# Gate columns by one full transposition a tile, products on all rows, and the sample read as the last 32 of 128 tokens

## The chip, the cores and the metric

The kernel runs on one core of a Trainium2 chip. The metric is the device time of one execution in microseconds (us), the median of several runs; lower is better. The engines are TensorE (PE in the profile, PEld for its loads of the stationary operand), VectorE (DVE), ScalarE (ACT), GpSimd (POOL) and SyncE (SP), which issues the DMAs.

## What is computed

One step of a streaming encoder layer for two streams at once: 1024 tokens of a new stream (the prompt) and the next 32 tokens of a running one (the sample). The mixer has three groups of heads, each a recurrence over the tokens that is computed in chunks; behind it comes a feed-forward part with a causal convolution. The reference, cut to what the change touches:

```python
proj = xn @ w_in                       # xn: (tokens, 1024)
(gq, gk, gv, gg, gr, hq, hf, hi, hg, mq, mk, mv, mi, mf, mo) = jnp.split(proj, pts, axis=-1)
log_a = log_sigmoid(gg @ gla_w_gate + gla_b_gate) / GLA_GATE_NORM      # gg: 16 columns
...
ig = mi + ml_b_i                       # 5 columns: input gate of the mLSTM heads
log_fm = log_sigmoid(mf + ml_b_f)      # 5 columns: forget gate
...
dc = jnp.exp(b[:, -1] + m - m_last)    # decay of a head's state over a chunk
c_new = dc[..., None, None] * c + jnp.einsum('bjh,bjhk,bjhv->bhkv', wk, kc, vc)
```

## The kernel before

**Tiling.** Tokens are worked on in three groups of 384, 384 and 256 prompt tokens, the last with the 32 sample tokens behind them (288 columns). A tile of tokens ("unit" u) has 128 tokens; the sample is unit 8 with n = 32. The function inproj makes the projections of a group: products with features in rows (pf, lines 350 and following), and products with tokens in rows (pv, lines 420 to 430). All large products are made of three passes over operands that are split into a high and a low part (mm3, lines 88 to 91), so lines 89, 90 and 91 carry most of TensorE's stream.

**Gate columns.** The first token-row product of a unit has 282 columns: 256 values, 16 gate columns gg, and 5 + 5 of the mLSTM gates. Line 428 copies the last 26 to tgs (tokens in rows, 26 columns a unit). Lines 471 to 473 turn them: for each unit three products of tgs with the identity put 16 columns on rows 64 to 79 of tg, and 5 each on rows 96 and 32 onwards. Lines 474 to 476 copy these rows to gg (which shares its tile with the forget gate fm) and ig.

**Products with few rows.** Line 529 multiplies gg (rows 64 to 79) with the gate weights into z0; line 604 does it for the other 64 channels into z3. Line 582 spreads the five decays dc over 128 rows. A product with few rows or columns uses a part of TensorE's array (a shape of rows x columns, such as 32x128 or 64x64).

**Mixers.** For each unit, mixer computes scores and states with many products of 64 rows and columns (line 776, sc, um, sm, up, og, oh). Lines 762 to 766 transpose the decayed keys kh, lines 794 to 802 those of the mLSTM heads, and lines 958 to 962 take row sums (mi at line 672; the helper first at line 671 issues all of these). In group 2 the later token-row products are made the other way round and transposed back at line 438 (pb), also for the sample's 32 tokens. Line 1405 transposes the result of the last part.

**The order.** The program is written unit by unit, but function order at the end lets a list scheduler (play) put the instructions of every engine in a new order, by estimated costs and tail lengths. Its function choose decides when TensorE leaves the full shape for a smaller one: small products wait until 300 ns of them have come together (GATE) or one has waited for PATIENCE, 3000 ns. So an edit in one place moves instructions elsewhere.

## Time and profile before

| | |
|---|---|
| median of 3 runs | 1328.19 us (1327.99 to 1331.88) |
| the profiled execution's own time | 1327.83 us |
| its span, first to last instruction | 1326.0 us |
| TensorE, TensorE's loads | 1293.3 us, 1208.7 us (98%, 91%) |
| VectorE, ScalarE, GpSimd | 1034.2, 724.8, 181.1 us |
| DMA over the span | 285.25 MB, 215 GB/s |

The share of busy time says which engine is full: TensorE. A product's duration in the profile runs from its start to its modelled end, and products overlap, so the time that one takes in the stream is the distance from its start to the next start. In a row of the timeline stand start, duration, engine, line, operation, what it writes and reads, the size of the stationary operand (rows\*columns), the moving operand, and the count of rows that were merged; in brackets the engine's idle time before it and what ended it.

### The profile page before, as it was taken

Reading aid. Unit: us, or ns where it says so; the run is one execution under the profiler, and the core shown is the slowest. Engines: PE = TensorE matmul, PEld = TensorE weight load, DVE = VectorE, ACT = ScalarE, POOL = GpSimd, SP = SyncE. Lnnn points to the kernel's source line nnn. Section 1 sums busy time; section 2 is a strip of 40 time slices with the busy share of each in tenths; the row PEclk is TensorE's granted clock in tenths of the full one; section 3 lists DMA queues with packets and bytes.
Section 4 is the critical chain, followed back from the end, with each engine's and each line's share of the span. In section 5 each row is a group of like instructions: output and inputs, shape, how many; then the busy total and the mean of one; then the engine's idle time right before and its main releaser. Section 6 shows DMA issues by size and latency. Waiting matters only on the chain. (4 is left out here: it accounts for less than half of the span.)

```text
span 1326.0 us, 30530 instructions
## 1 busy us (share of the span) xinstructions
PE 1293.3 (98%) x12005; PEld 1208.7 (91%) x12005; DVE 1034.2 (78%) x1877; ACT 724.8 (55%) x1432; POOL 181.1 (14%) x331
## 2 busy tenths in 40 slices
PE   8999999999998999999999999999999999999997
PEld 7999999999898888778899999999999999888886
DVE  6795559748788478779899998888888878676686
ACT  6555566546576454436754545445454455365664
POOL 2020001111011112223112211111111110010010
PEclk9999999999999999999999999999999999999999
DMA  9899879977899863545256643222232268887774
GB/s 333 283 337 334 268 264 317 318 252 247 279 317 297 307 234 116 176 119 157 104 191 195 217 153 121 95 99 81 90 121 97 97 217 286 295 273 259 226 251 179
DMA packets 148455, 285.25 MB, mean 215 GB/s; under 512 B 30071, under 2 KB 84503, under 8 KB 148311
## 3 DMA queue, kind: packets, MB, share of 16 engines
q1 hardware_dynamic: 148311, 283.30, 63.7%
q8 instruction: 94, 1.54, 0.5%
q14 instruction: 50, 0.41, 0.1%
HBM read 201.90 MB, written 81.34 MB: 214 GB/s over the span
## 5 line engine op out<-in xcount | busy, mean ns | idle before, releaser
L1257 DVE SCALAR_TENSOR_TENSOR y<-uu,fconv_sb,y 128x1060 f32<-128x1060 f32 x88 | 116.0, 1321 | 7.7 <-ACT y L1255 6.7
L98 DVE TENSOR_TENSOR hlp<-rp,hhp 128x384 fp32r<-128x384 f32 x77 | 42.5, 555 | 35.3 <-PE pdw L91 11.3
L1255 ACT ACTIVATE y<-uu,fconv_sb 128x1060 f32<-128x1060 f32 x44 | 56.2, 1277 | 22.9 <-POOL uu L1252 17.1
L95 ACT CAST hhp<-rp 128x384 fp32r<-128x384 f32 x77 | 39.6, 515 | 49.0 <-PE pdx L90 18.2
L1203 ACT COPY c<-pux 128x274 f32<-128x274 f32 (+1 forms) x132 | 46.2, 380 | 27.1 <-PE pux L91 25.0
L933 POOL TENSOR_TENSOR hrs<-hss,mhalf 128x5 f32<-128x5 f32 (+3 forms) x27 | 36.1, 1340 | 163.8 <-DVE hss L932 162.8
L98 DVE TENSOR_TENSOR wdp<-rp,wdp 128x512 fp32r<-128x512 f32 x77 | 52.0, 688 | 3.7 <-ACT wdp L95 2.6
L89 PE MATMUL pv<-wt_0h,xh 128*128 128x256 f32 (+2 forms) x195 | 53.1, 294 | 1.4 <-ACT xh L311 0.6
L95 ACT CAST wdp<-rp 128x512 fp32r<-128x512 f32 x77 | 47.0, 621 | 10.1 <-PE pdx L91 3.4
L91 PE MATMUL pv<-wt_0h,xl 128*128 128x256 f32 (+2 forms) x195 | 50.6, 286 | 0.2 <-DVE xl L312 0.2
L90 PE MATMUL pv<-wt_0l,xh 128*128 128x256 f32 (+2 forms) x195 | 50.4, 284 | 0.2 <-DVE wt_0l L98 0.2
L91 PE MATMUL pv<-wt_1h,xl 128*128 128x256 f32 (+2 forms) x195 | 48.1, 287 | 0.0
L89 PE MATMUL pv<-wt_1h,xh 128*128 128x256 f32 (+2 forms) x195 | 47.2, 285 | 0.0
L90 PE MATMUL pv<-wt_1l,xh 128*128 128x256 f32 (+2 forms) x195 | 46.9, 285 | 0.0
L1252 POOL COPY uu<-fcache_sb 128x2 f32<-128x2 f32 x44 | 19.0, 431 | 185.8 <-DVE uu L1208 185.8
L91 PE MATMUL pdx<-wdp,hlp 128*128 128x512 f32 x132 | 43.2, 391 | 0.0
L90 PE MATMUL pdx<-wdp,hhp 128*128 128x512 f32 x132 | 43.0, 389 | 0.0
L89 PE MATMUL pdx<-wdp,hhp 128*128 128x512 f32 x132 | 42.7, 391 | 0.0
L1254 POOL COPY fhalo<-uu 128x2 f32<-128x2 f32 x44 | 35.7, 812 | 50.5 <-DVE uu L1208 49.9
L89 PEld LDWEIGHTS pv<-wt_0h,xh 128*128 128x128 f32 (+1 forms) x195 | 34.8, 187 | 2.8 <-ACT xh L311 0.9
L211 POOL TENSOR_SCALAR gss<-gss 128x1 f32<-128x1 f32 (+1 forms) x9 | 6.7, 747 | 216.6 <-ACT gjk L1331 132.5
L91 PEld LDWEIGHTS pv<-wt_0h,xl 128*128 128x128 f32 (+1 forms) x195 | 34.3, 187 | 1.0 <-issue 0.4
(1784 smaller groups left out, 5124.4 us busy)
## 6 DMA issues: line engine op xcount, KB each, us to landing
h_d<-y SPq DMA_DIRECT2D x22, 530.0 KB, 3.3
rp<-t_d SPq DMA_DIRECT2D x44, 256.0 KB, 3.9
wt_0r<-in_w_tok SPq DMA_DIRECT2D x21, 512.0 KB, 6.1
wt_1r<-in_w_tok SPq DMA_DIRECT2D x21, 512.0 KB, 5.5
rp<-in_w_dn SPq DMA_DIRECT2D x33, 256.0 KB, 4.2
rp<-s_d SPq DMA_DIRECT2D x44, 192.0 KB, 3.8
wt_0l<-lt_d SPq DMA_DIRECT2D x14, 512.0 KB, 5.0
wt_1l<-lt_d SPq DMA_DIRECT2D x14, 512.0 KB, 5.6
```

The source lines that it names most:

```text
L89: pe.matmul(ps, lh[0], rh[0], start=first, stop=False, **kw)
L90: pe.matmul(ps, lh[0], rh[1], start=False, stop=False, **kw)
L91: return pe.matmul(ps, lh[1], rh[0], start=False, stop=last, **kw)
L95: act.copy(hi, src)
L98: (eng or pool).tensor_tensor(lo, src, hi.bitcast(F32), op=ALU.subtract)
L211: pool.tensor_scalar(out, ss, other, EPS, op0=ALU.add, op1=ALU.add)
L933: pool.tensor_tensor(rs[:n, h0:h0 + nh], ss[:n, h0:h0 + nh], mhalf[:n, :nh], op=ALU.pow)
L1203: act.copy(t, ps)
L1252: pool.tensor_copy(u[:, GAP_S:GAP_S + 2], fcache[:, j, :])
L1254: pool.tensor_copy(fhalo[:, j, :], u[:, NCOL - 2:NCOL])
L1255: act.activation(y, u, AF.Identity, scale=fconv[:, j, 2:3], bias=fconv[:, j, 3:4])
L1257: dve.scalar_tensor_tensor(y, uu[i][:, s:s + NCOL], fconv[:, j, s:s + 1], y, op0=ALU.mult, op1=ALU.add)
```

## The change

The gate columns are kept as 128 columns a unit, zero but for the 26 in use, each set already at the column that will be its row: ScalarE copies 16 to columns 64 to 79, VectorE the other ten to columns 32 and 96 onwards, and GpSimd fills the tile with zeros first. One transposition a unit then writes all 128 rows of tg. The tile now uses the buffers of tag "q", two of them. The gate products read 96 rows (the weights of the other rows are zero) and write 128; the decay product reads 128 rows, with dc filled with zeros.

For the sample, products that read its 32 tokens now read 128 tokens, of which its own are the last 32 (in line 1405 and in the row sums the first 32), so that they use the full shape; the rest of the result is not read. Its keys are transposed at once, as 128 columns of four planes, and copied in four pieces. PATIENCE goes to 4000. The diff, cut:

```diff
         def vg_store(blk, u, off, n, ps):
+            r = slice(128 - n, 128)
...
-                act.copy(o[:n], ps[:n, :256])
-                sp.dma_start(v_d[t:t + n, 256 * blk:256 * blk + 256], o[:n])
+                act.copy(o[r], ps[r, :256])
+                sp.dma_start(v_d[t:t + n, 256 * blk:256 * blk + 256], o[r])
...
-                    mm3(ps[:n, :N], (xh[:, k, off:off + n], xl[:, k, off:off + n]), ws[k], k == 0, k == 7)
+                    mm3(ps, (xh[:, k, off + n - 128:off + n], xl[:, k, off + n - 128:off + n]), ws[k], k == 0, k == 7)
                 if not blk:
-                    act.copy(tgs[:n, i, :], ps[:n, 256:])
+                    act.copy(tgs[:, i, 64:80], ps[:, 256:272])
+                    dve.tensor_copy(tgs[:, i].rearrange("p (a b) -> p a b", b=64)[:, :, 32:37],
+                                    ps[:, 272:282].rearrange("p (a b) -> p a b", b=5))
...
-                        pe.transpose(ps[:n, 128 * e:128 * e + 128], fs[e][:, off:off + n], ident)
+                        pe.transpose(ps[:, 128 * e:128 * e + 128], fs[e][:, off + n - 128:off + n], ident)
...
-        tgs = pf.tile([128, 3, 26], F32, tag="tgs", name=f"tgs{g}")
+        tgs = pf.tile([128, 3, 128], F32, tag="q", name=f"tgs{g}", bufs=2)
+        pool.memset(tgs, 0.0)
...
-            for (r0, c0, c1) in ((64, 0, 16), (96, 16, 21), (32, 21, 26)):
-                pe.matmul(gt_[r0:r0 + c1 - c0, off:off + n], tgs[:n, i, c0:c1], ident[:n, :n], start=True, stop=True)
-        act.copy(gg[64:80], gt_[64:80, :T])
+            pe.transpose(gt_[:, off + n - 128:off + n], tgs[:, i], ident)
+        act.copy(gg[:96], gt_[:96, :T])
...
-        pe.matmul(z0[:, :T], wg[64:80, 0:128], gg[64:80, :], start=True, stop=True)
+        pe.matmul(z0[:, :T], wg[:96, 0:128], gg[:96], start=True, stop=True)
...
+            pool.memset(dc, 0.0)
...
-                pe.matmul(dcp[:, f, :ci], self_[R, 128 * f:128 * f + 128], dc[R, :ci], start=True, stop=True)
+                pe.matmul(dcp[:, f, :ci], self_[:, 128 * f:128 * f + 128], dc[:, :ci], start=True, stop=True)
...
-        pe.matmul(z3[:64, :T], wg[64:80, 128:192], gg[64:80, :], start=True, stop=True)
+        pe.matmul(z3[:, :T], wg[:96, 64:192], gg[:96], start=True, stop=True)
...
-        for f0 in (0, 2):
+        if u == 8:
+            kps = small(128)
+            pe.transpose(kps, khf, ident)
+            for f in range(4):
+                act.copy(kt[:n, 128 * f:128 * f + 128], kps[n * f:n * f + n])
+        for f0 in (0, 2) if u < 8 else ():
...
+        if u == 8:
+            dve.memset(z[:, 128:224], 0.0)
         for f in range(4):
-            first(pe.matmul, sd[:n], z[:, f * n:f * n + n], of_head[:, f, :], start=f == 0, stop=f == 3)
+            first(pe.matmul, sd, z[:, f * n:f * n + 128], of_head[:, f, :], start=f == 0, stop=f == 3)
...
-                    pe.transpose(pts[hf][:n, 128 * d:128 * d + 128], accs[4 * hf + d][:, off[u]:off[u] + n], ident)
+                    pe.transpose(pts[hf][:, 128 * d:128 * d + 128], accs[4 * hf + d][:, off[u]:off[u] + 128], ident)
...
-GATE, PATIENCE = 300., 3000.
+GATE, PATIENCE = 300., 4000.
```

Where TensorE's order moves, in three places. First, in group 0, the first gate columns (tg from tgs) behind the transpositions of the third unit's input (xt) and among that unit's token-row products (pv). Before (the last two rows then follow once more, for the second unit, and behind them line 91):

```order
L309 MATMUL xt_318<-ident,x_107 128x128 x4
L89 MATMUL pv_0_325<-wt_0_0h,xh_185 128x282
L90 MATMUL pv_0_325<-wt_0_0l,xh_185 128x282
L473 MATMUL tg_356<-ident,tgs_202 16x128
L473 MATMUL tg_356<-ident,tgs_202 5x128 x2
```

Now:

```order
L91 MATMUL pv_0_284<-wt_0_2h,xl_186 128x282
L309 MATMUL xt_321<-ident,x_107 128x128 x4
L89 MATMUL pv_0_328<-wt_0_0h,xh_185 128x282
L90 MATMUL pv_0_328<-wt_0_0l,xh_185 128x282
L91 MATMUL pv_0_328<-wt_0_0h,xl_186 128x282
```

The first gate transposition now stands nine rows further down, and the second some 26 rows behind that. Line 91, which reads xl, comes directly behind line 90.

Second, the end of the same group's last gate columns and the product z0 that reads them (pf are feature-row products). Before:

```order
L90 MATMUL pf_8_376<-xl_186,wf_8h 128x384
L91 MATMUL pf_8_376<-xh_185,wf_8l 128x384
L473 MATMUL tg_356<-ident,tgs_202 16x128
L473 MATMUL tg_356<-ident,tgs_202 5x128 x2
L529 MATMUL z_0_419<-r_fm_354,wg_sb 128x384
L89 MATMUL pf_6_433<-xh_185,wf_6h 128x384
```

Now:

```order
L90 MATMUL pf_8_374<-xl_186,wf_8h 128x384
L91 MATMUL pf_8_374<-xh_185,wf_8l 128x384
L476 MATMUL tg_360<-ident,tgs_202 128x128
L532 MATMUL z_0_417<-r_fm_358,wg_sb 128x384
L89 MATMUL pf_6_431<-xh_185,wf_6h 128x384
```

Three rows became one; z0 follows directly in both.

Third, the sample's keys (kh) in group 2, among token-row products pv, transpositions back (pb) and the sample's small products (sm). Before:

```order
L91 MATMUL pv_5_1_6621<-xh_4321,wt_5_1l 128x288
L672 MATMUL mi<-ident,kh_7017 32x128 x2
L438 MATMUL pb_4_6647<-ident,vf_6503 128x128 x2
L438 MATMUL pb_4_6655<-ident,vf_6503 32x128 x2
L776 MATMUL sm_7027<-mqk_6902 32x32 x3
L776 MATMUL sm_7028<-mqk_6902 32x32 x2
L89 MATMUL pv_6_0_6676<-xh_4321,wt_6_0h 128x288
```

Now:

```order
L441 MATMUL pb_5_6699<-ident,vf_6583 128x128
L90 MATMUL pv_6_0_6673<-xl_4320,wt_6_1h 128x288
L91 MATMUL pv_6_0_6673<-xh_4319,wt_6_1l 128x288
L768 MATMUL mi<-ident,kh_7014 128x128
L89 MATMUL pv_6_1_6707<-xh_4319,wt_6_0h 128x288
```

The keys' one transposition stands alone among wide products; the small products sm went to a later place, together with the sample's state products.

## The prediction

> **What bounds the kernel now.** I read the page first, then busy time by stage, then the waits of the engine that is full, and last the timeline of TensorE alone around every line that the change touches.

> ```profile
> span 1326.0 us, 30530 instructions
> PE 1293.3 (98%) x12005; PEld 1208.7 (91%) x12005; DVE 1034.2 (78%) x1877; ACT 724.8 (55%) x1432; POOL 181.1 (14%) x331
> ```

> The span is TensorE's: it is busy for 1293 of 1326 us. So an edit counts only as far as it shortens TensorE's stream of products or moves a wait in it. The profiled execution took 1327.83 us, 1.8 us more than its span and 0.36 us less than the median of the runs shown (1328.19); the sum below is made against 1327.83. A measurement of this kernel can tell about 0.3% (4 us) from no change, so the line for "faster" lies at 1324.2 and for "slower" at 1332.2.

> ```profile
> 0.00:400.00 400.00, 391.55 (x4594) 372.88 (x4595) 288.63 (x625) 238.52 (x471) 46.63 (x82) 1.00 0.88 296
> 400.00:480.00 80.00, 72.23 (x981) 65.61 (x980) 55.30 (x148) 45.02 (x111) 7.93 (x7) 0.98 0.83 278
> ```

> Each row has the stretch, its length, busy time and instructions of PE, PEld, DVE, ACT and POOL, then TensorE's granted clock (full, or 0.98 of it), the DMA engines' share and GB/s. TensorE is idle for 8.4 us of the first 400 and for 7.8 us of the 80 after that, where the sample's mixer runs and the DMA engines are 83% busy. Of the second half of the program the change touches eight transpositions (line 1405) and nothing else, so I look at the first. The waits that concern the change are short:

> ```profile
> PE pv L91 <- DMA wt_1l<-lt_d: 1.8, 1, 1.8
> PE tg L473 <- DVE xl L312: 1.4, 2, 0.9
> PE z L529 <- ACT r_fm L474: 0.7, 1, 0.7
> ```

> **Gate columns (lines 428 and 471 to 476).** Per tile three narrow products of two passes each go, and one transposition comes. In the timeline (start, duration) the next start shows what a row costs, since products overlap:

> ```profile
> 163.61 0.29 PE L90 MATMUL pv<-wt_2l,xh 128*128 128x282 f32 x1
> 163.74 0.29 PE L91 MATMUL pv<-wt_2h,xl 128*128 128x282 f32 x1
> 163.96 0.61 PE L473 MATMUL tg<-ident,tgs 128*16 128x128 f32 x12
> 164.50 0.44 PE L89 MATMUL pf<-xh,wf_8h 128*128 128x384 f32 x1
> 164.78 0.33 PE L90 MATMUL pf<-xl,wf_8h 128*128 128x384 f32 x1
> ...
> 167.76 0.33 PE L89 MATMUL pf<-xh,wf_8h 128*128 128x384 f32 x1
> 168.03 0.40 PE L473 MATMUL tg<-ident,tgs 128*16 128x128 f32 x6
> 168.35 0.44 PE L90 MATMUL pf<-xl,wf_8h 128*128 128x384 f32 x1
> 168.64 0.34 PE L91 MATMUL pf<-xh,wf_8l 128*128 128x384 f32 x1
> ```

> From 163.74 to 164.78 pass 1.04 us, in which the two wide products need 0.13 (163.61 to 163.74) and 0.18 (384 columns; 42.91 to 43.08 below has 0.17): a group for two tiles costs 0.73. From 167.76 to 168.64 pass 0.88, less twice that: a group for one tile costs 0.52. What a full transposition costs is seen at line 588:

> ```profile
> 110.86 0.28 PE L91 MATMUL pv<-wt_1h,xl 128*128 128x256 f32 x1
> 110.98 0.27 PE L588 MATMUL mi<-ident,r_st 128*128 128x128 f32 x1
> 111.01 0.36 PE L89 MATMUL pv<-wt_0h,xh 128*128 128x256 f32 x1
> 111.33 0.28 PE L91 MATMUL pv<-wt_0h,xl 128*128 128x256 f32 x1
> ```

> From 110.86 to 111.33 are 0.47 us; three wide products of 0.12 stand in them (lines 91, 89 and, left out here, 90): it costs 0.11, the reload of the stationary operand behind it included. Three groups of tokens make 3 x 1.25 = 3.75 before and 9 x 0.11 = 0.99 after. One place gives nothing back: in the first group the third transposition stands, as before, right ahead of the gate product, and TensorE waits there for ScalarE's copy of the gate rows (0.7 us in the list of waits). I leave out the 0.4 us of that place: **-2.4 us** (bounds -1.5 to -2.8).

> The two waits for xl at line 473 look as if they went with it. They don't:

> ```profile
> 20.98 1.28 DVE L312 TENSOR_TENSOR xl<-xt,xh 128x512 fp32r<-128x512 f32 x2
> 21.71 0.61 PE L473 MATMUL tg<-ident,tgs 128*16 128x128 f32 x12 [0.88 <-DVE xl L312]
> ```

> The product behind the group reads the xl that VectorE finishes at about 21.6. In the new order it stands directly behind line 90 of the same tile (the rows stand in the section on the change), and inherits the 0.88 us. The same holds for the other 0.5 us unless the four small products that now stand ahead of it fill it. I count these waits unchanged.

> **Gate and decay products (lines 529, 604, 582).** The work is the same, on all rows.

> ```profile
> 42.91 0.34 PE L90 MATMUL pf<-xl,wf_3h 128*128 128x384 f32 x1
> 43.08 0.33 PE L91 MATMUL pf<-xh,wf_3l 128*128 128x384 f32 x1
> 43.34 0.85 PE L604 MATMUL z<-r_fm,wg_sb 16*64 16x384 f32 x2
> 44.13 0.45 PE L89 MATMUL pf<-xh,wf_2h 128*128 128x384 f32 x1
> 44.42 0.34 PE L90 MATMUL pf<-xl,wf_2h 128*128 128x384 f32 x1
> ...
> 101.37 0.28 PE L91 MATMUL pv<-wt_1h,xl 128*128 128x256 f32 x1
> 101.58 0.83 PE L582 MATMUL mi<-r_dc,cf_sb 5*128 5x6 f32 x6
> 102.34 0.39 PE L89 MATMUL pv<-wt_0h,xh 128*128 128x256 f32 x1
> 102.56 0.28 PE L90 MATMUL pv<-wt_0l,xh 128*128 128x256 f32 x1
> ...
> 256.34 0.95 PE L672 MATMUL mi<-cf_sb,x 128*128 128x11 f32 x8
> 257.15 0.37 PE L91 MATMUL pv<-wt_0h,xl 128*128 128x256 f32 x1
> ```

> A product for z3 costs 1.34 - 0.35 = 0.99 us. The first start comes 0.09 late (0.26 behind line 91 where 0.17 is usual): the array changes its shape. That goes, and the second pass no longer waits for its own load, about 0.10 (the pace of the eight short passes at 256.34, 0.81 / 8). I take 0.2 a piece for z3, and 0.13 for z0, two of which follow small products and don't pay the change of shape twice: **-1.0** for six (bounds -0.3, the shape alone, and -2.5, if a full-row pass cost what a wide 384-column row does). The decay product costs 1.19 - 0.24 = 0.95; six passes at the pace of 256.34 take 0.61 and a reload 0.08, so 0.26 go, once only 0.1: **-0.6** (0 to -0.9).

> **The sample.** Its four key transpositions become one:

> ```profile
> 458.92 0.29 PE L91 MATMUL pv<-xh,wt_1l 128*128 128x288 f32 x1
> 459.05 0.38 PE L672 MATMUL mi<-ident,kh 128*32 128x128 f32 x2
> 459.36 0.30 PE L776 MATMUL up<-v,kt 32*32 32x64 f32 x4
> 459.60 0.66 PE L438 MATMUL pb<-ident,vf 128*128 128x128 f32 x4
> ...
> 488.93 0.42 PE L672 MATMUL mi<-cf_sb,x 128*32 128x11 f32 x8
> 489.28 0.33 PE L1033 MATMUL ctp<-ident,ct 128*128 128x128 f32 x1
> ```

> Three fewer at 0.11: **-0.33**. The row sums (line 961) go from 32 to 128 stationary columns: eight passes take 0.35 us from 488.93 to 489.28, and 0.81 in the full form at 256.34: **+0.46**. [...] The widened products of lines 426 and 438 cost nothing more: their loads hide behind streams of 282 or 128 columns, and

> ```profile
> L438 PE MATMUL pb<-ident,vf x42: 269/272/415, 404.4 to 472.3; 128*128 128x128 f32 x28, 128*32 128x128 f32 x14
> ```

> narrow and full transpositions have one duration. On the other engines come nine VectorE copies, three GpSimd fills, a VectorE fill and two more ScalarE copies, each a fraction of a microsecond on an engine that is 14 to 78% busy. Their cover is TensorE's backlog; where a copy stood last before a transposition its own length would be paid, at most 9 x 0.2 = 1.8.

> **The new order.** Counted over both orders, trips into a smaller shape of the array fall from 71 to 66, but ten were made by the removed lines alone and are in the terms above. The small products of the mixers now take 66 trips for 61. A trip costs at least the 0.09 us between 459.27 (where the next row was due) and 459.36, and at most the 0.33 us from 459.27 to 459.60 with its four products; I take 0.25: **+1.25** for five (0.45 to 1.65).

> The sum: -2.4 - 1.0 - 0.6 - 0.33 + 0.46 + 1.25 = -2.6, so 1327.83 - 2.6 = **1325.2 us**.

> **Rivals.** (a) *Every change of tile shape costs.* The narrow products at column 0 (lines 438, 672, 1405, the sample's rows of line 426) are another shape, too; with them shape changes fall from 194 to 150, 31 of these beyond those counted. At half a trip, 0.125 us, that is 3.9 more: 1321.3. Against it stands the row of line 438, equal durations, and the 0.22 us that two narrow ones take from 459.05. For it: line 473, whose narrow products lie at other columns, does pay. [...] Chance 0.13.

> (b) *The waits go as well.* 7.8 us of idle time between 400 and 480 us hang on the sample's key transpositions and their copies, and line 473's waits on a place in the order. If about half went: 1325.2 - 5 = 1320. Nothing in the old trace says that the new order waits less; chance 0.20.

> (c) *Absorbed.* If the loads set the pace where line 91 waited 1.8 us for wt_1l, what was gained before is waited for there; only -0.33 + 0.46 is left: 1328.0. Against it: in the first 400 us the DMA engines are 88% busy, not full. Chance 0.12.

> (d) *Slower.* The patience before a change of shape goes from 3000 to 4000, so the mixers' products come later; between 400 and 480 us the sample's chain is already late. If the idle time there doubles, +7.8 - 2.6 gives 1333.0; it decides from 7 us of new idle time on. DVE's new copies, which wait for TensorE with other work queued behind them, would push the same way. Chance 0.08.

> That the change doesn't do what it says is ruled out: the new order has no product of 16 or 5 columns left.

> **How the numbers follow.** The sum holds with 0.47; its own range is 1322 to 1328 by the bounds, and a fifth of it (0.09) lies under 1324.2. Faster: 0.09 + 0.13 + 0.20 = 0.42. Within: 0.38 + 0.12 = 0.50. Slower: 0.08. The range for 8 in 10 reaches from 1318 (both a and b in part) to 1331.

> **What would show it.** Line 476 with nine transpositions of 0.11 us each; z3 at 0.8 instead of 0.99; a wait of 0.9 us for xl, now at line 91, near 21 us; the wait for the gate rows near 30 us still there; row sums of the sample at 0.8; idle time between 400 and 480 us near 8 us. Were a narrow transposition at column 0 a change of shape, the rows around line 441 would close up by more than 0.1. The forecast is wrong if that idle time moves by more than 3 us.

## The result, and the profile after

The changed kernel takes 1320.49 us (median of 7 runs, 1317.65 to 1321.63) where the kernel before took 1326.9 in the same comparison: a ratio of 0.9937, 95% interval 0.9919 to 0.9955. A second comparison (12 runs of it, 29 of before) gave 0.9956 (0.9939 to 0.9973). So it is faster by about half a per cent, 6 to 8 us, where the forecast was 1325.2. The sum's own range ended at 1322; the range for 8 in 10, with the rivals in it, at 1318.

The first lines of the page of the changed kernel, then its busy time by stage (columns as in the prediction):

```profile
span 1318.7 us, 30445 instructions
PE 1288.4 (98%) x11957; PEld 1208.1 (92%) x11957; DVE 1035.0 (78%) x1887; ACT 723.9 (55%) x1434; POOL 185.5 (14%) x337
```

```profile
0.00:400.00 400.00, 390.27 (x4557) 375.77 (x4558) 293.27 (x638) 238.77 (x474) 46.95 (x89) 1.00 0.90 300
400.00:480.00 80.00, 78.21 (x1057) 71.24 (x1054) 56.98 (x155) 47.34 (x116) 7.78 (x7) 1.00 0.85 293
```

The span is 7.3 us shorter: TensorE is 4.9 us less busy and 2.4 us less idle. The idle time between 400 and 480 us, which the prediction watched, fell from 7.8 to 1.8. And the granted clock of that row is 1.00 now; before it was 0.98, in a row that the prediction quoted and passed over. TensorE's waits between 400 and 480 us, before (longest five) and after:

```profile
PE pv L91 <- DMA wt_1l<-lt_d: 1.8, 1, 1.8
PE oh L776 <- issue: 1.4, 1, 1.4
PE pb L438 <- ACT vf L450: 1.0, 1, 1.0
PE pb L438 <- DVE vg L415: 0.9, 2, 0.7
PE zp L89 <- ACT vth L101: 0.9, 1, 0.9
```

```profile
PE pv L89 <- ACT vf L453: 1.1, 2, 0.7
PE zp L90 <- DVE wo6l L1020: 0.4, 1, 0.4
PE pv L89 <- DVE vg L416: 0.2, 1, 0.2
```

These old waits had five different releasers, a DMA among them. Three of them (for the DMA, for ScalarE's vth, and the one of oh), 4.1 of these 6.0 us, are not on lines that the change touches.

**What the clock costs.** Busy time by stretches of 3.41 us in the kernel before, cut where the clock changes (the last three columns are the clock, DMA share and GB/s):

```profile
448.16:451.57 3.41, 1.88 (x19) 1.32 (x20) 2.28 (x9) 3.19 (x9) 0.74 (x1) 1.00 0.95 309
451.57:454.98 3.41, 3.41 (x17) 3.39 (x16) 0.30 (x1) 0.00 (x0) 0.00 (x0) 0.50 1.02 386
639.31:642.72 3.41, 1.33 (x6) 0.91 (x7) 3.41 (x4) 2.86 (x4) 0.00 (x0) 1.00 0.01 2
642.72:646.13 3.41, 3.41 (x18) 3.41 (x17) 3.41 (x4) 2.46 (x4) 0.00 (x0) 0.50 0.00 0
```

In the first and the third window TensorE waited for 1.5 and 2.1 of 3.41 us. Behind each comes a window at half clock, in which it is busy throughout and does little more than half the work: in the kernel before, a pass of 288 columns starts 240 ns behind the one ahead in such windows and 132 ns elsewhere, one of 256 columns 213 and 119 ns (medians). So about 1.5 us of the 3.41 are lost, and the busy time hides it. The kernel before has four such windows inside the program (at 342, 452, 540 and 643 us), the changed one three (13, 532, 535).

With that, each profiled execution can be cut into three, from the starts of TensorE's products: **idle** is the sum of the gaps between products (the bracketed ones of the timeline and the shorter ones, 0.4 to 0.9 us in all); **half clock** is half of the busy time that falls in windows at 0.50, 1.7 us a window, a little more than the 1.5 that it costs; the **stream** is the rest between the start of the first product and that of the last, about TensorE's work at full clock. From 9.1 to 9.9 us lie outside. (The first transpositions of the changed kernel, of line 233, start 213 ns apart up to the trace's first mark of the clock, at 5.86 us, and 111 ns apart behind it; by this pace the first ran at half clock too, but they are counted to the stream.)

In the table, in us, stand these parts with the median time and the ratio to before of the same comparison. The last column is taken not from the profile but from every execution whose granted clock is on record: the share of the clock that was not granted times the span, the mean over the runs (107 of before, 9 with PATIENCE 4000, 7 and 12 of the changed kernel, 12 of each of the others). It counts a window at 1.7 too, and of it 1.2 to 2.8 us lie behind the last product in the profiles.

| kernel | time | ratio (95%) | span | stream | idle | half clock | clock lost, all runs |
|---|---|---|---|---|---|---|---|
| before | 1326.9 | 1 | 1326.0 | 1286.1 | 23.2 | 6.8 | 9.3 |
| before, again | 1329.4 (1 run) | | 1327.6 | 1285.4 | 24.7 | 7.9 | |
| changed | 1320.5 | 0.9937 (0.9919 to 0.9955) | 1318.7 | 1283.5 | 21.1 | 4.5 | 6.0 |
| changed, again | 1320.5 | 0.9956 (0.9939 to 0.9973) | 1316.6 | 1284.0 | 21.3 | 1.7 | 5.6 |
| changed, PATIENCE 3000 | 1328.5 | 1.0019 (1.0001 to 1.0037) | 1327.0 | 1283.8 | 25.3 | 8.5 | 9.5 |
| changed, PATIENCE 5000 | 1333.5 | 1.0047 (1.0029 to 1.0065) | 1328.6 | 1282.7 | 28.1 | 8.1 | 11.8 |
| changed, z0 and z3 on 16 rows | 1330.0 | 1.0033 (1.0015 to 1.0052) | 1327.8 | 1286.2 | 25.2 | 6.7 | 9.3 |
| changed, old sample mixer | 1326.1 | 0.9992 (0.9969 to 1.0014) | 1327.2 | 1283.5 | 26.0 | 8.2 | 7.1 |
| changed, old row sums | 1322.8 | 0.9974 (0.9956 to 0.9993) | 1320.3 | 1283.2 | 22.7 | 5.0 | 6.5 |
| changed, first filling | 1322.4 | 0.9967 (0.9946 to 0.9988) | 1318.8 | 1284.6 | 21.1 | 3.4 | 5.9 |
| changed, second filling | 1320.3 | 0.9949 (0.9933 to 0.9965) | 1321.1 | 1285.1 | 19.9 | 6.4 | 4.5 |
| before, PATIENCE 4000 | 1332.0 | 1.0046 (1.0026 to 1.0065) | 1328.6 | 1288.7 | 25.7 | 5.1 | 7.2 |
| before, gate columns alone | 1330.4 | 1.0019 (0.9999 to 1.0039) | 1331.4 | 1285.7 | 24.8 | 11.4 | 9.4 |
| before, 32 columns as full shape | 1327.1 | 1.0001 (0.9981 to 1.0022) | 1326.9 | 1286.0 | 23.6 | 8.2 | 7.7 |

From the mean of before's two executions to that of the changed kernel's two, the stream falls by 2.0 us, idle time by 2.8 and half clock by 4.3; with 1.5 us for a window it is 2.5 for the stream and 3.8 for half clock. The stream is the prediction's sum (-2.6). These two pairs of executions differ by 9.1 us, more than the kernels do. Over 107 and 19 executions the spans differ by 6.7 us (means), and of these 3.5 (95% interval 2.5 to 4.5) are clock that was not granted, or some 3.1 at the price above. So the larger part of the gain is what the prediction held fixed, and about half of it is the half clock.

### The profile page after: what moved, and what is told of

Its sections match the earlier page's. It is cut to its first block, busy times and chain, and to the rows that moved or that the text cites. A ratio compares the mean times of both kernels' runs of the same rounds, so it can differ in the third digit from the quotient of the medians.

```text
span 1318.7 us, 30445 instructions
## 1 busy us (share of the span) xinstructions
PE 1288.4 (98%) x11957; PEld 1208.1 (92%) x11957; DVE 1035.0 (78%) x1887; ACT 723.9 (55%) x1434; POOL 185.5 (14%) x337
## 5 line engine op out<-in xcount | busy, mean ns | idle before, releaser
L1272 DVE SCALAR_TENSOR_TENSOR y<-uu,fconv_sb,y 128x1060 f32<-128x1060 f32 x88 | 115.9, 1320 | 10.3 <-ACT y L1270 9.4
L89 PE MATMUL pv<-wt_0h,xh 128*128 128x256 f32 (+1 forms) x195 | 51.7, 293 | 3.0 <-DVE xl L312 1.3
L90 PE MATMUL pv<-wt_0l,xh 128*128 128x256 f32 (+1 forms) x195 | 49.8, 284 | 0.2 <-DVE wt_0l L98 0.2
L91 PE MATMUL pv<-wt_0h,xl 128*128 128x256 f32 (+1 forms) x195 | 49.8, 285 | 0.2 <-DVE xl L312 0.2
L1267 POOL COPY uu<-fcache_sb 128x2 f32<-128x2 f32 x44 | 24.5, 557 | 175.7 <-DVE uu L1223 175.7
L89 PE MATMUL pv<-wt_1h,xh 128*128 128x256 f32 (+1 forms) x195 | 48.1, 287 | 0.0
L91 PE MATMUL pv<-wt_1h,xl 128*128 128x256 f32 (+1 forms) x195 | 47.9, 289 | 0.0
L90 PE MATMUL pv<-wt_1l,xh 128*128 128x256 f32 (+1 forms) x195 | 47.6, 289 | 0.0
L90 PE MATMUL pdx<-wdp,hhp 128*128 128x512 f32 x132 | 43.2, 390 | 0.0
L91 PE MATMUL pdx<-wdp,hlp 128*128 128x512 f32 x132 | 43.1, 391 | 0.0
L89 PE MATMUL pdx<-wdp,hhp 128*128 128x512 f32 x132 | 42.7, 391 | 0.0
L89 PEld LDWEIGHTS pv<-wt_0h,xh 128*128 128x128 f32 x195 | 34.5, 188 | 4.2 <-DVE xl L312 1.6
L90 PEld LDWEIGHTS pv<-wt_0l,xh 128*128 128x128 f32 x195 | 34.4, 189 | 0.5 <-DVE wt_0l L98 0.4
```

Of the source, the lines that this page charges most:

```text
L89: pe.matmul(ps, lh[0], rh[0], start=first, stop=False, **kw)
L90: pe.matmul(ps, lh[0], rh[1], start=False, stop=False, **kw)
L91: return pe.matmul(ps, lh[1], rh[0], start=False, stop=last, **kw)
L1267: pool.tensor_copy(u[:, GAP_S:GAP_S + 2], fcache[:, j, :])
L1272: dve.scalar_tensor_tensor(y, uu[i][:, s:s + NCOL], fconv[:, j, s:s + 1], y, op0=ALU.mult, op1=ALU.add)
```

## The experiments

Three theories at the start: the gain is TensorE's work and the waits were only shifted (A); the sample's part removed the waits between 400 and 480 us (B); the longer patience made a better order (C).

**Patience alone, on both sides**

```diff
-GATE, PATIENCE = 300., 3000.
+GATE, PATIENCE = 300., 4000.
```

in the kernel before:

> The kernel before with PATIENCE 4000 and nothing else. Theory A (terms: most of the gain is less work in TensorE's stream, and the idle time of the old order was merely shifted about): the stream keeps its length, so the time stays within 4 us of before. Theory B (the sample's part removed the idle time between 400 and 480 us): also within 4 us, and that idle time stays near 7.8 us. Theory C (the longer patience made a better order): faster by 5 us or more, and the idle time between 400 and 480 us falls from 7.8 to under 4 us.

and the reverse in the changed kernel:

> The changed kernel with PATIENCE back at 3000. A and B: as the changed kernel, 6 to 8 us faster than before, give or take 2. C: at most 3 us faster than before, and the idle time around 400 to 480 us is back above 6 us.

Measured: 1.0046 (slower by 4 us by the medians, 6 by the ratio) and 1.0019. C fails by the first. A, too, misses there, as the stream alone is some 3 us longer (1288.7), and the idle time between 400 and 480 us fell to 5.6, without the sample's part. A and B fail by the second: with all its other parts in place the changed kernel loses its whole gain, though its stream (1283.8) is what it was. Idle time is 4 us longer and half clock costs 5 us more in the profiled execution, 3.7 more over all.

**z0 and z3 on 16 rows again**

```diff
-        pe.matmul(z0[:, :T], wg[:96, 0:128], gg[:96], start=True, stop=True)
+        pe.matmul(z0[:, :T], wg[64:80, 0:128], gg[64:80], start=True, stop=True)
...
-        pe.matmul(z3[:, :T], wg[:96, 64:192], gg[:96], start=True, stop=True)
+        pe.matmul(z3[:64, :T], wg[64:80, 128:192], gg[64:80], start=True, stop=True)
...
```

> The changed kernel with z0 and z3 made from 16 rows again, as before. A: the two products (12 passes) take 4.5 us of TensorE's stream again where the changed kernel needs 2.1, so the time is 2.5 us above the changed kernel's. The prediction's own step (0.13 and 0.2 us a product) would give 1.0 us. B and C: no more than those 1.0 us, the idle time as in the changed kernel.

The stream is 2.5 us longer (1286.2 against 1283.7), as A had it, though the order alone moves a stream by as much (1288.7 above). The time went up by some 10 us, as no theory had it; the rest is again idle time (+4.0) and half clock (+3.6). TensorE's timeline around z3, first of this kernel, then of the changed one:

```profile
45.35 0.34 PE L90 MATMUL pf<-xl,wf_3h 128*128 128x384 f32 x1
45.62 0.85 PE L608 MATMUL z<-r_fm,wg_sb 16*64 16x384 f32 x2
46.41 0.44 PE L89 MATMUL pf<-xh,wf_2h 128*128 128x384 f32 x1
46.68 0.34 PE L90 MATMUL pf<-xl,wf_2h 128*128 128x384 f32 x1
```

```profile
42.12 0.34 PE L91 MATMUL pf<-xh,wf_3l 128*128 128x384 f32 x1
42.30 0.81 PE L608 MATMUL z<-r_fm,wg_sb 96*128 96x384 f32 x2
42.65 0.63 PE L89 MATMUL pf<-xh,wf_2h 128*128 128x384 f32 x1
43.12 0.34 PE L89 MATMUL pf<-xh,wf_3h 128*128 128x384 f32 x1
```

From the product ahead to the second one behind pass 1.33 and 1.00 us; less the two wide ones (0.35) z3 costs 0.98 and 0.65.

**The sample's mixer as before**

```diff
-        if u == 8:
-            kps = small(128)
-            pe.transpose(kps, khf, ident)
...
-        for f0 in (0, 2) if u < 8 else ():
+        for f0 in (0, 2):
...
-            first(pe.matmul, sd, z[:, f * n:f * n + 128], of_head[:, f, :], start=f == 0, stop=f == 3)
+            first(pe.matmul, sd[:n], z[:, f * n:f * n + n], of_head[:, f, :], start=f == 0, stop=f == 3)
```

(head transpositions and line 1405 likewise)

> The changed kernel with the sample's mixer as before: four key transpositions, head transpositions on 32 tokens, row sums with 32 stationary columns, and 32-column transpositions at the end. A: 0.33 up and 0.46 down in the stream, so within 2 us of the changed kernel. B: the idle time of the stretch in which the sample's mixer runs comes back to 6 us or more, and the time is 4 to 6 us above the changed kernel's.

0.9992: the gain is gone, as B wanted, but not by B's waits. TensorE is idle for 3.7 us between 400 and 480 us, not for 6 or more, and for 4.8 us more than in the changed kernel over the whole program. The stream is unchanged. The half clock costs 5 us more in the profiled execution, but over all executions only 1.3 more, which is within the noise.

This left a fourth theory (D): the stream is 2 to 3 us shorter by the change's own work; idle time and half clock hang on the whole order of instructions, which the planner makes anew after any edit, and on where the windows fall. Four runs tested it.

**Both kernels once more**

> The changed kernel itself once more, beside the others of this call. Theory D (its full-clock stream is 2.6 us shorter than before; what it gains beyond that is idle time and half-clock windows, which hang on the order of the instructions and on where the free-running 3.41 us windows fall): the full-clock stream is 1283.5 us again and the idle time 21 us, both within 1, since order and waits are the program's own; only the number of half-clock windows differs, by one or two at 1.7 us each; time 1318 to 1322 us, ratio 0.993 to 0.996. If instead the idle time moves by more than 2 us from one execution to the next, the order doesn't set it.

> The kernel before itself, one look. D: full-clock stream 1286.1 us, idle time 23 us, both within 1; the half-clock windows (four inside the program in the first profile) may be two to five, and at other places, though each stands behind a window with idle time in it.

As D said: stream and idle time repeat within 0.7 and 1.5 us (the latter a little over what was expected), the half-clock windows don't. The changed kernel has one (at 632 us) where it had three, the kernel before five where it had four.

**The gate columns alone, in the kernel before**

```diff
...
-            for (r0, c0, c1) in ((64, 0, 16), (96, 16, 21), (32, 21, 26)):
-                pe.matmul(gt_[r0:r0 + c1 - c0, off:off + n], tgs[:n, i, c0:c1], ident[:n, :n], start=True, stop=True)
+            pe.transpose(gt_[:, off:off + n], tgs[:n, i], ident[:n, :n])
```

> The kernel before with the gate columns alone turned by a full transposition (the sample's from its 32 rows). The term of the sum: gate columns 2.67 us of stream down to about 0.6, so the full-clock stream is 2.1 us shorter than before. D: that much of stream, and a time anywhere within 5 us of before, since idle time and windows are redrawn with the order. A theory that the whole gain hangs on the gate columns (rival b, their waits go too): 5 us or more faster than before.

1.0019, so the gain doesn't hang on this part. A miss for the stream: the gate columns themselves take 0.8 us where they took 2.7, but the mixers' small products take 73.0 where they took 70.6, and the stream is as long as before. Even the work at full clock changes by 2 us with the order, through what these small products take.

**Patience 5000 in the changed kernel**

> The changed kernel with PATIENCE 5000. D: the full-clock stream stays within 1 us of 1283.5, and the time lies between 1320 and 1331, most likely above the changed kernel's, because idle time and half-clock windows are drawn anew. Theory C (longer patience is better with the new shapes): as fast as the changed kernel or faster, and idle time 21 us or less.

1333.5 us, slower than before by 0.47% and outside D's range for the time; the stream is 1282.7. C fails again. A row of busy time by stretches shows where a good part went:

```profile
400.00:480.00 80.00, 75.33 (x1016) 69.74 (x1015) 61.62 (x162) 47.48 (x113) 10.66 (x8) 0.96 0.87 289
442.60:446.01 3.41, 0.70 (x4) 0.38 (x4) 2.27 (x10) 1.46 (x7) 0.00 (x0) 1.00 0.74 234
446.01:449.42 3.41, 3.41 (x15) 3.10 (x15) 1.45 (x5) 3.39 (x12) 0.70 (x1) 0.50 0.74 210
```

2.7 us of idle time stand in one window at 442.6, and a window at half clock follows.

**Old row sums, and another view of shapes.** In the changed kernel line 976 goes back to 32 stationary columns (the last lines of the sample's diff above). In the kernel before, the planner takes products of 32 columns at column 0 for the full shape, so that they are no longer held back; no product changes:

```diff
-    if mode == (128, 128) or (mode == (128, 32) and not f32) or mode == (32, 128):
+    if mode == (128, 128) or (mode == (128, 32) and (not f32 or not c)) or mode == (32, 128):
```

> The changed kernel with the sample's row sums on 32 stationary columns again, as before. The term of the sum: the eight passes take 0.46 us less, so the full-clock stream is 0.5 us below the changed kernel's 1283.7. D: the order changes over a long stretch, so idle time and windows are drawn anew: time between 1318 and 1330, more likely above the changed kernel's than below.

> The kernel before, with products of 32 columns at column 0 no longer taken for a change of shape where the order is made (they were held back until 300 ns of them had come together). No product changes. A theory that the new order gained by this freedom: full-clock stream or idle time falls by 3 us or more, faster than before by 4 us. D, and the prediction's view that such products cost no change of shape: full-clock stream 1285.8 within 1.5, the rest drawn anew, time within 5 us of before.

Both as D had it. The old row sums take 0.37 us (468.86 to 469.23 in its timeline) where the changed kernel's take 0.89, the term as predicted. The stream falls by as much (1283.2 against 1283.7), but two executions of one kernel differ by that, too. The kernel comes out 2 us behind the changed one. The freer planner gains nothing (1.0001).

**Filling a wait.** All executions share a group of waits at the start of the feed-forward part, the first of them for T1 in most orders; a window at half clock stood behind it in 12 of the 13 executions in which it stayed (not in ten, as the second expectation below counts). Eight products whose results are overwritten go into it; they read line 1223's sum:

```diff
+        if f == 0 and n == 256:
+            for i in range(8):
+                pe.matmul(w[:, :128], ident, uu[0][:, 2 + o:130 + o], start=True, stop=True, skip_group_check=True)
         product(w, "p5", W, X, True, True)
```

> The changed kernel with eight products whose results are overwritten, placed in the wait for T1 at the start of the feed-forward part (about 632 us; 2.6 us of idle time in 3.5 us stand there in every execution so far). All before them keeps its order. D, with the rule that a 3.41 us window with much idle time is followed by one at half clock (price 1.7 us): full-clock stream up by 1.8 us, idle time down by about 1.5, and no half-clock window between 628 and 656 us, where nine of the ten executions so far had one or two. Time as the changed kernel's or up to 2 us less, as the changed kernel has a window there in some executions only. If the half-clock windows have nothing to do with idle time, they come there as often, and the time goes up by what the eight products add beyond the wait.

The filling failed: the sum that it reads came 2.73 us after TensorE had run dry, so the idle time stood in one piece, and the window came. Busy time by window:

```profile
631.10:634.50 3.40, 1.21 (x10) 1.22 (x11) 3.40 (x5) 2.96 (x5) 1.21 (x2) 1.00 0.01 2
634.50:637.90 3.40, 3.40 (x18) 3.40 (x17) 3.40 (x4) 1.99 (x2) 2.12 (x2) 0.50 0.00 0
```

The second filling has twelve products and reads `c1[:, :128]`, an earlier copy:

> The changed kernel with twelve products whose results are overwritten (24 passes, 2.7 us at full clock), this time reading the copy of an earlier sum, which is ready when the wait for T1 begins; the first try read a tile that came only with T1 itself, so its wait stayed whole. D with the rule that idle time brings a half-clock window: the waits near 632 us fall from 2.6 us to under 1, no half-clock window between 628 and 656 us, full-clock stream 1283.7 + 2.7, idle time about 2 us below 21, span within 2 us of the changed kernel's other executions and 1.7 below those that had the window there. If idle time has no part in the windows, one comes there as in ten of the thirteen executions so far. A window near 12, 444, 483 or 531 us may come or not, and says nothing of this.

Its timeline and its busy time by window:

```profile
635.24 0.28 PE L91 MATMUL puy<-B21h,A_0h 128*128 128x256 f32 x1
635.36 2.84 PE L1235 MATMUL puw<-c,ident 128*128 128x128 f32 x24
637.95 0.36 PE L89 MATMUL puw<-T1h,S_0h 128*128 128x256 f32 x1
```

```profile
630.50:633.91 3.41, 2.75 (x21) 2.30 (x20) 3.15 (x5) 3.41 (x12) 0.00 (x0) 1.00 0.04 11
633.91:637.32 3.41, 3.37 (x29) 3.38 (x30) 2.99 (x3) 3.41 (x8) 0.00 (x0) 1.00 0.01 2
637.32:640.73 3.41, 2.81 (x22) 2.38 (x21) 3.41 (x5) 1.78 (x3) 0.00 (x0) 1.00 0.00 0
```

The wait is filled and no window at half clock follows, for which D and its rule about idle time stand. It is one execution, and the changed kernel's first had none there either. Over 12 executions each, 4.5 us of clock are lost with the second filling, 5.9 with the first and 5.8 without; that points the same way, but is not clear of chance. In this execution windows came elsewhere (13, 16, 535, 555 us), the stream is 1.4 us longer, not 2.7, and the time is that of the changed kernel (0.9949). No version tried beats it by more than the measurement can tell.

## Why the prediction was right in its sum and short of the result

**Gate columns: right.** A transposition between wide products costs 0.11 as forecast. In the timeline after, the third row starts 0.24 us after the transposition, of which the second takes 0.13:

```profile
162.60 0.27 PE L476 MATMUL tg<-ident,tgs 128*128 128x128 f32 x1
162.63 0.37 PE L90 MATMUL pv<-wt_1l,xh 128*128 128x282 f32 x1
162.84 0.33 PE L89 MATMUL pf<-xh,wf_8h 128*128 128x384 f32 x1
```

**The waits at this place: right in kind.** They stayed, longer if anything: 1.35 us for xl (at line 89, not 91) and 0.56 us for the gate rows, 0.88 and 0.7 before.

```profile
22.91 0.40 PE L89 MATMUL pv<-wt_0h,xh 128*128 128x282 f32 x1 [1.35 <-DVE xl L312]
31.46 0.91 PE L532 MATMUL z<-r_fm,wg_sb 96*128 96x384 f32 x2 [0.56 <-ACT r_fm L477]
```

The 0.55 us for xl at 325 us went. The idle time of the first 400 us is 9.7 where it was 8.4.

**z0 and z3: mis-sized.** "I take 0.2 a piece for z3" was 0.33 (0.98 to 0.65 above). The 0.13 for z0 was 0.20 where TensorE waits ahead of it (from its start to that of the second wide product behind it: 1.12 us from 30.68 before, 0.92 from 31.46 after) and 0.30 at the next place (1.12 from 171.61, 0.82 from 170.22). So the six make -1.6 to -1.9, not -1.0. The experiment's -2.5 of stream, the outer bound, has a new order in it.

**Decay product and row sums: right.** From 433.73 to 434.91 pass 1.18 us, less three wide products (0.39) and the transposition among them (0.11): the six passes on full rows cost 0.68 where they cost 0.95, 0.27 less for 0.26 forecast. The sample's row sums take 0.89 (465.58 to 466.47), the change of shape behind them included, for 0.81 forecast:

```profile
433.73 0.30 PE L91 MATMUL pv<-xh,wt_1l 128*128 128x288 f32 x1
433.86 0.27 PE L441 MATMUL pb<-ident,vf 128*128 128x128 f32 x1
433.89 0.38 PE L89 MATMUL pv<-xh,wt_0h 128*128 128x288 f32 x1
434.11 0.73 PE L586 MATMUL mi<-r_dc,cf_sb 128*128 128x5 f32 x6
434.69 0.38 PE L90 MATMUL pv<-xl,wt_0h 128*128 128x288 f32 x1
434.91 0.30 PE L91 MATMUL pv<-xh,wt_0l 128*128 128x288 f32 x1
...
465.58 0.96 PE L676 MATMUL mi<-cf_sb,x 128*128 128x11 f32 x8
466.47 0.43 PE L785 MATMUL sc<-Qz,qkb 64*32 64x32 f32 x16
```

**Trips into smaller shapes: right in the number, the price not borne out.** The mixers' small products (the tiles sc, og, oh, up, um, sm and oi) take 72.0 us of stream where they took 70.6, 1.4 more; the term was +1.25. The traces count 60 trips into the shapes of line 776's products before and 65 after, five more as forecast. But with the gate columns alone there are 62 and the products take 2.4 us more, and with the old row sums also 62 and they take 72.0. So 0.25 us a trip came out by luck, and the term isn't the change's own.

**Rival (a) is refuted.** The transpositions of line 441, 14 of them narrow before, all full now, take the time they took, and their rows haven't closed up. In the kernel before, the next product starts 109 ns behind a narrow one of line 438 and 109 behind a full one, and 131 ns behind both kinds with 282 columns (medians). After:

```profile
L441 PE MATMUL pb<-ident,vf x42: 270/273/329, 400.8 to 463.8; 128*128 128x128 f32 x42
```

The shape changes of this kind went, as (a) said, and the stream shows nothing for them beyond the terms: its 2.0 to 2.6 us leave no room for 3.9 more.

**Rivals (c) and (d).** The wait of 1.8 us for wt_1l, on which (c) stood, went, and the gain wasn't absorbed there. The idle time between 400 and 480 us fell where (d) had it double; but the price of the longer patience that (d) feared shows in the kernel before, which is 4 to 6 us slower with it.

**The step that failed** is the one that the sum stands on: that idle time stays as it was ("Nothing in the old trace says that the new order waits less"). It fell by 6 us between 400 and 480 us. By the prediction's own sign ("wrong if that idle time moves by more than 3 us") this step is wrong. Of the 6 us about 1 came back before 400 and 2 between 480 and 620 us (busy time before, then after):

```profile
480.00:620.00 140.00, 137.02 (x1476) 109.18 (x1475) 111.87 (x213) 71.18 (x162) 31.85 (x39) 0.99 0.50 155
480.00:620.00 140.00, 135.13 (x1443) 107.53 (x1441) 112.24 (x207) 71.29 (x162) 36.09 (x43) 0.98 0.43 142
```

The wait for T1 kept its 1.5 us. Net, 2.4 us are left. The second half of the failure is that the half clock wasn't in the sum at all. It was worth as much again in the first execution (2.3 us), and 3.5 us over all executions on record. Rival (b), with its 1320, had the size, and half of the mechanism. Its place was right, its cause was not: undoing the sample's part brings back 1.9 us of idle time there, but so do edits that don't touch the sample (5.0 us idle there with patience 3000, 4.7 with 5000). And in the kernel before, edits that leave the sample's part alone lower it from 7.8 and 7.0 in its two executions to 5.6 (patience 4000), 4.6 (gate columns) and 4.4 (the freer planner).

What is shown is that less idle time belongs to this order as a whole: it repeats in a second execution, and four edits of the changed kernel, two of them of nothing but the order, lose it. Why the planner's order happens to wait less here is open. No single wait explains it, and the plan's own view of these waits wasn't compared with the trace. The smaller half-clock loss lasts over the executions (6.0 and 5.6 us of clock in the two comparisons, 9.3 before).

## What to carry to other kernels

Cut a profile of a kernel bound by TensorE into stream, idle time and half clock before any sum; the busy share hides the third (a window at 0.50 shows TensorE busy for 3.41 of 3.41 us). Where a planner makes the order, any edit draws the waits of the whole program anew, by up to 13 us here: judge a part by its own rows and the stream, and a version by its time, run again. Waits that clumped cost more than their length here: the 2.1 us in one window ahead of 642.72 were followed by a window at half clock, in which 1.5 more were lost.

## What the runs showed of the hardware that wasn't expected

No single wait had to fill a window: in these executions two or three waits of 0.5 to 1.5 us in one were enough (ahead of 642.72 in the kernel before, waits of 1.48, 0.66 and 0.50 us, with 2.1 us of them in the window).
